# Fourteen matmul units of each half's mixing stage, regrouped into seven pairs with a seven product scheme

## The chip, the cores and the metric

One core of one Trainium2 chip runs the whole kernel in one launch. The metric is device time in microseconds (us), the median of the runs shown; a profile of one execution stands beside it. PE is TensorE (matrix multiply), PEld its weight loads, DVE is VectorE, ACT is ScalarE, POOL is GpSimd, SP is SyncE, whose queue issues most DMAs.

## The reference

One decoder layer on x (2048 tokens, 1024 features), all in float32:

```
u = rmsnorm(x, norm_mix_w);  proj = u @ w_in          # 1024 -> 2048 + 768 columns
q, f, v, g: 4 heads x 128 columns each;   att: 8 query heads, 2 key/value heads of 64
f = lb + (1 - lb) * sigmoid(f);  k = 1 - f;  q = q * 128**-0.5
S_t = diag(f_t) S_{t-1} + k_t v_t^T;  o_t = S_t^T q_t          # a recurrence per head
o_hg  = rmsnorm(o) * hg_norm_w * silu(g)
o_att = sliding window attention (128 keys back), with a sink logit per head
h = x + concat(o_hg, o_att) @ w_out
h = h + (silu(conv3(v2 @ w_gate)) * (v2 @ w_up)) @ w_down      # v2 = rmsnorm(h), d_ff = 2816
out = rmsnorm(h, final_norm_w)
```

## The kernel before

Everything lies transposed: features on 128 partitions, tokens along the free dimension. The 2048 tokens go in two halves (`hf`) of 1024. For each half there are four stages: the mix (projections, recurrence, attention), `out_proj`, `gate_up` and `down`. The first half's X is made in `head`, the second's at the end of the first half's `down`.

A float32 matrix product is made from three float32r products: an operand is split into a rounded `hi` (an ACT cast) and the rest `lo` (a DVE subtraction), and hi·hi, hi·lo and lo·hi are summed in PSUM. X, the eight K tiles of the normed input (128x1024 each), is held split in `xh`/`xl`.

`unit` (L204) is the plain projection of 128 columns: `prep` (L195) loads 512 KB of weights into `raw`, splits it into `whi`/`wlo`, and 8 K tiles x 3 products x 2 column halves = 48 matmuls of 128x512 fill two PSUM banks (line L222). In the mix of a half, 15 units run: `q` of attention (four, in `attend`, L493), `f` and `hq` of the recurrence (L586, L591; the `f` of head 0 is made earlier and comes in as `fu`), and `g`, the gate (L628). `project_v` (L782) makes the values of all four heads with 192 matmuls (L792 to L794) into one tile `v` of 16 KB a partition. PSUM has eight banks: four of kind `mm` for units, two `hg` for the recurrence, two `at` for attention.

`hgrn` (L584) is the recurrence of a head: seven doubling levels (L669 to L722), each with a multiply in place on DVE (L683), a gathering copy on ACT (L679) and small matmuls (L665), then the states (L743), the output (L757, L758), its norm and the gate. `QK`, `f`, `strip` and `SS` have one buffer each, so that the heads follow one another. `attend` (L491) is a pair of attention heads: scores (L520), masks (L529), exponentials (L542), transposes (L556) and outputs (L569). Both are generators that yield after each step. The string `ORDER` (L47) writes the order of the steps by hand: H0 is the next step of head 0, A1 of attention pair 1, W and V are the weights and the run of `project_v`, G1 the early weights of a gate, and S splits six of the eight tiles of the mix into operands for `out_proj`. The tile scheduler then places instructions by that priority: on PE, an instruction of an earlier step goes first as soon as it can, and a later one fills in where it can't. Tail: `out_proj` begins with the six tiles from S while head 3 and attention pair 3 finish.

Buffers: `raw` has three (`RAW`), `whi` and `wlo` two each. The pool `h` has eight 4 KB slots under the tag `m` (`slot`, L346), for the whole kernel; the six finished mix tiles wait in them until S.

`gate_up` already uses a seven product scheme (Strassen's, in Winograd's form) over all K tiles in `pair_unit` (L959), with its ACT copies of partial sums (L982).

## Time and profile before

| What | Value |
|---|---|
| three timed runs | 2113.6, 2114.18, 2114.54 us (median 2114.18) |
| span of the profiled execution, first to last instruction | 2112.5 us |
| PE, DVE, ACT busy over the span | 99%, 77%, 52% |
| mean TensorE clock granted | 0.999 |
| first half: mix from the end of the first `f` unit to the last mix instruction | 43.4 to 366.7 us |
| of it `project_v` | 65.9 to 111.5 us |

The page gives no time of its own for the profiled execution beside its span; the span lies 1.7 us under the median of the timed runs, for the start and the end of the launch. Times of instructions are from the span's start. A matmul's busy time overlaps with that of the next, so PE's pace is read from the time of many matmuls in a row and not from the mean of one.

### The profile page before, as it was taken

The page shows a single profiled execution, that of the slowest core. Times are in us where ns is not written, and L with a number is a line of the kernel's source. Part 1 is how long each engine was busy: PE and PEld are TensorE (multiplying, and loading weights), DVE is VectorE, ACT ScalarE, POOL GpSimd, SP SyncE. Part 2 cuts the span into 40 slices and gives each one's busy share as a digit, 9 for nine tenths or more (in the row PEclk, how much of TensorE's full clock was granted, in tenths as well). Part 3 has the DMA queues.
Part 4 walks back from the last instruction along what each step waited for, and adds up shares of the span by engine and source line. Part 5 has one row for each costly group of instructions (what it writes and reads, how often), then busy time and mean ns, then how long its engine had stood idle before and what let it go on. Part 6 is the DMA issues. An engine that isn't in the chain of part 4 may idle for free.

```text
span 2112.5 us, 29613 instructions
## 1 busy us (share of the span) xinstructions
PE 2098.0 (99%) x11480; PEld 1740.9 (82%) x11480; DVE 1624.3 (77%) x2355; ACT 1088.1 (52%) x1877; POOL 24.6 (1%) x52
## 2 busy tenths in 40 slices
PE   9999999999999999999999999999999999999998
PEld 7888888888888888888888888888888888888887
DVE  7457887898888878786773677868988788887766
ACT  6365565664444445345744566656544444444354
POOL 2000000000000000000000000000000000000000
PEclk9999999999999999999999999999999999999999
DMA  4111111513332325964641111214233233269643
GB/s 161 42 51 34 33 42 53 175 60 115 102 122 86 119 96 185 389 213 157 218 134 52 31 34 35 77 45 149 80 100 130 88 102 120 85 217 385 230 149 135
DMA packets 96617, 255.19 MB, mean 121 GB/s; under 512 B 17370, under 2 KB 19802, under 8 KB 96476
## 3 DMA queue, kind: packets, MB, share of 16 engines
q1 hardware_dynamic: 91220, 251.45, 34.9%
q10 hardware_dynamic: 5256, 1.85, 0.3%
q8 instruction: 90, 1.47, 0.3%
q14 instruction: 51, 0.42, 0.1%
HBM read 195.11 MB, written 57.16 MB: 119 GB/s over the span
## 4 chain that ended last, share of the span: by engine, by line
PE 96%; ACT 2%; DMA 1%; DVE 1%; issue 0%; SPq 0%; DVEq 0%
PE X L975 8%; PE X L976 8%; PE X L977 8%; PE pop L222 7%; PE hq L222 4%; PE q L222 4%; PE f L222 4%; PE pdx L1193 4%; PE pdx L1194 4%; PE pdx L1195 4%; PE Y L977 4%; PE Y L976 4%; PE Y L975 4%; PE g L222 3%; PE pdy L1194 3%; PE pdy L1193 3%
## 5 line engine op out<-in xcount | busy, mean ns | idle before, releaser
L800 ACT CAST whi<-raw 128x1024 fp32r<-128x1024 f32 x88 | 92.6, 1052 | 110.0 <-PE X L976 74.1
L975 PE MATMUL X<-T,whi 128*128 128x512 f32 x352 | 137.4, 390 | 0.0
L976 PE MATMUL X<-T,whi 128*128 128x512 f32 x352 | 137.0, 389 | 0.0
L977 PE MATMUL X<-T,wlo 128*128 128x512 f32 x352 | 137.0, 389 | 0.0
L1074 DVE SCALAR_TENSOR_TENSOR y<-ga,cw,y 128x1024 f32<-128x1024 f32 x88 | 112.3, 1278 | 25.7 <-ACT y L1072 25.7
L201 DVE TENSOR_TENSOR wlo<-raw,whi 128x1024 fp32r<-128x1024 f32 x57 | 69.3, 1218 | 60.8 <-ACT whi L200 60.5
L982 ACT COPY u<-X 128x512 f32<-128x512 f32 x88 | 51.6, 587 | 121.4 <-PE X L977 121.3
L801 DVE TENSOR_TENSOR wlo<-raw,whi 128x1024 fp32r<-128x1024 f32 x88 | 107.1, 1217 | 2.1 <-ACT whi L800 2.1
L200 ACT CAST whi<-raw 128x1024 fp32r<-128x1024 f32 x57 | 59.6, 1048 | 77.9 <-PE q L222 22.3
L222 PE MATMUL pop<-XL,whi 128*128 128x512 f32 x256 | 88.8, 391 | 0.0
L222 PE MATMUL pop<-XH,whi 128*128 128x512 f32 x256 | 88.0, 393 | 0.0
L222 PE MATMUL pop<-XH,wlo 128*128 128x512 f32 x256 | 87.1, 390 | 0.0
L801 DVE TENSOR_TENSOR xld<-raw,xhd 128x1024 fp32r<-128x1024 f32 x72 | 80.2, 1129 | 8.7 <-ACT xhd L800 8.6
L679 ACT COPY G<-QK 128x1024 f32<-128x1024 f32 x48 | 51.4, 1071 | 66.7 <-DVE QK L683 45.5
L800 ACT CAST xhd<-raw 128x1024 fp32r<-128x1024 f32 x72 | 68.9, 978 | 27.0 <-DMA raw<-act1B 6.0
L975 PEld LDWEIGHTS X<-T,whi 128*128 128x128 f32 x352 | 66.0, 188 | 15.1 <-ACT u L982 1.6
L977 PEld LDWEIGHTS X<-T,wlo 128*128 128x128 f32 x352 | 66.1, 188 | 13.8
L976 PEld LDWEIGHTS X<-T,whi 128*128 128x128 f32 x352 | 66.1, 188 | 13.7
L683 DVE TENSOR_TENSOR QK<-QK,f 128x1024 f32<-128x1024 f32 x56 | 68.5, 1223 | 11.3 <-ACT G L679 11.1
L1194 PE MATMUL pdx<-xld,hid 128*128 128x512 f32 x192 | 74.7, 389 | 0.0
L1193 PE MATMUL pdx<-xhd,hid 128*128 128x512 f32 x192 | 74.2, 390 | 0.0
L1195 PE MATMUL pdx<-xhd,lod 128*128 128x512 f32 x192 | 72.4, 389 | 0.0
(393 smaller groups left out, 6280.6 us busy)
## 6 DMA issues: line engine op xcount, KB each, us to landing
wr<-in_w_down SPq DMA_DIRECT2D x90, 512.0 KB
raw<-in_w_gate SPq DMA_DIRECT2D x44, 512.0 KB
raw<-in_w_up SPq DMA_DIRECT2D x44, 512.0 KB
raw<-act0T SPq DMA_DIRECT2D x20, 512.0 KB
raw<-act1T SPq DMA_DIRECT2D x20, 512.0 KB
act0B<-y SPq DMA_DIRECT2D x33, 256.0 KB
act1B<-y SPq DMA_DIRECT2D x33, 256.0 KB
raw<-in_w_out SPq DMA_DIRECT2D x16, 512.0 KB
```

The lines of the kernel that those rows point to most:

```text
L201: nc.vector.tensor_tensor(lo, raw, hi.bitcast(F32), op=ALU.subtract)
L222: marks["unit"] = nc.tensor.matmul(o[b], w, x[:, bs], start=f, stop=l)
L683: done = nc.vector.tensor_tensor(own, own, Fv.rearrange("p b w -> p w b").unsqueeze(3).to_broadcast([P, 2, nb, m]), op=ALU.mult)
L800: return (nc.scalar.copy(h, src), (eng or nc.vector).tensor_tensor(l, src, h.bitcast(F32), op=ALU.subtract))
L801: (eng or nc.vector).tensor_tensor(l, src, h.bitcast(F32), op=ALU.subtract))
L975: nc.tensor.matmul(o, wh[:, ws], xh, start=i == 0 and not more, stop=False, skip_group_check=more)
L976: nc.tensor.matmul(o, wh[:, ws], xl, start=False, stop=False, skip_group_check=more)
L977: r = nc.tensor.matmul(o, wl[:, ws], xh, start=False, stop=i == 3, skip_group_check=more)
L1074: nc.vector.scalar_tensor_tensor(y, g[:, w:w + HALF], C.cw[:, ft, w:w + 1], y, op0=ALU.mult, op1=ALU.add)
L1193: nc.tensor.matmul(o, wh[:, i, c], ah[:, i, cols], start=f, stop=False, skip_group_check=more)
L1194: nc.tensor.matmul(o, wh[:, i, c], al[:, i, cols], start=False, stop=False, skip_group_check=more)
L1195: nc.tensor.matmul(o, wl[:, i, c], ah[:, i, cols], start=False, stop=l, skip_group_check=more)
```

## The change

A pair of units with 256 output columns takes its first four K tiles as a 2x2 block product by seven products instead of eight, and its last four K tiles plainly. `Twofold` makes the combined halves of X once a half (T1 to T4, from X loaded anew), `two_units` runs a pair. The pairs are `q` of attention pair j with gate `g` of head j (four pairs), and `f` with `hq` of heads 1 to 3 (three pairs); `hq` of head 0 stays a plain unit. The gate is now made in `attend`, with ACT's Silu in place of a Sigmoid and a multiply. To make room, the slots `m` belong to each stage's pool (8 in the head, 5 in the mix, 8 in the rest), six finished mix tiles go to DRAM (`keep`) and come back at S, and the values of heads 1 to 3 go to DRAM and come back one at a time. The order is written anew, `project_v` now stands directly behind the unit of head 0. Core of the diff:

```diff
 ORDER = """
-H0 A0 H0 W0 V0 H0 G0 H0 A0 A0 H0 H0 H1 H0 H1 H1 H1 A0 A1 A0 G1 A1 A1 H1 H1 A1 A1 H2 H1 A2 H2 H2 H2 A2 H3 G2 A2 H2 A2 H2 A2 H2 A3 H3 H3 H3 A3 A3 H3 S A3 H3 A3 H3
+H0 W0 T0 H0 V0 U0 H0 A0 H0 H0 A0 A0 H0 H1 H0 H1 H1 H1 A1 H1 A0 A0 A1 A1 H1 H2 H1 A1 A1 H2 H2 H2 A2 H2 A2 A2 H2 H3 A2 A2 H2 H3 A3 H3 H3 A3 A3 H3 S A3 H3 A3 H3
 """
+DEEP = 2
+SLOTS = 5
+ROLES = ("XYZV", "ZYXV")
...
+    def keep(t, bs, name, kept, k):
+        if k not in kept:
+            kept[k] = dp.tile([P, HALF], F32, name=name)
+        nc.sync.dma_start(kept[k][:, bs], t[:, bs])
...
-        o = unit(a["w_att"][j], X, "q")
-        qT = slot(f"att{j}")
-        for b, bs in halves():
-            nc.vector.scalar_tensor_tensor(qT[:, bs], o[b], 0.125, invb[:, bs], op0=ALU.mult, op1=ALU.mult)
+        qT, g = slot(f"att{j}"), queries[j]
+
+        def scaled(bs):
+            nc.vector.scalar_tensor_tensor(qT[:, bs], qT[:, bs], 0.125, invb[:, bs], op0=ALU.mult, op1=ALU.mult)
             nc.scalar.activation(qT[:, bs], qT[:, bs], AF.Identity, bias=C.bq[:, j:j + 1])
+
+        def gated(bs):
+            nc.vector.tensor_tensor(g[:, bs], g[:, bs], invb[:, bs], op=ALU.mult)
+            nc.scalar.activation(g[:, bs], g[:, bs], AF.Silu)
+
+        two_units((a["w_att"][j], a["w_g"][j]), X, T, ((qT, scaled), (g, gated)))
...
-                mix[4 + j] = qT
+                keep(qT, gs, f"mix{hf}{4 + j}", mix, 4 + j)
...
+            two_units((a["w_f"][h], a["w_q"][h]), X, T, ((f, lambda bs: forget(bs, f[:, bs])),
+                                                         (q, lambda bs: scaled(bs, q[:, bs]))))
...
-        v = p.tile([P, HG, TT, P], F32, name="v")
+        v = [p.tile([P, TT, P], F32, tag=t, name=f"v{h}", bufs=n)
+             for h, (t, n) in enumerate((("v", 1), ("sc", 2), ("sc", 2), ("SS", 1)))]
...
-            nc.scalar.activation(v[:, :, tt], o.rearrange("p (h d) -> p h d", h=HG), AF.Identity,
-                                 scale=rs[:, tt:tt + 1])
+            for h in range(HG):
+                nc.scalar.activation(v[h][:, tt], o[:, h * P:(h + 1) * P], AF.Identity, scale=rs[:, tt:tt + 1])
+        away = {}
+        for h in range(1, HG):
+            away[h] = dp.tile([P, TT, P], F32, name=f"v{hf}{h}")
+            nc.sync.dma_start(away[h], v[h])
+
+        def values(h):
+            if h == 0:
+                return v[0]
+            t = p.tile([P, TT, P], F32, tag="v", name=f"v{h}", bufs=1)
+            nc.sync.dma_start(t, away[h])
+            return t
...
+    class Twofold:
...
+        def begin(self):
+            hf, p, lo, hi = self.hf, self.p, slice(0, 512), slice(512, HALF)
+            for i in range(DEEP):
+                x = []
+                for k in (i, i + DEEP):
+                    t = raw4(a["xT"][k, :, hf * HALF:(hf + 1) * HALF])
+                    nc.scalar.activation(t, t, AF.Identity, scale=nmw[:, k:k + 1])
+                    x.append(t)
+                x, y = x
+                t1 = p.tile([P, 512], F32, tag="pp", name="t1", bufs=4)
+                nc.vector.tensor_tensor(t1, x[:, hi], x[:, lo], op=ALU.subtract)
+                nc.vector.tensor_tensor(y[:, hi], y[:, hi], x[:, hi], op=ALU.subtract)
+                nc.vector.tensor_tensor(x[:, lo], y[:, hi], x[:, lo], op=ALU.add)
+                nc.vector.tensor_tensor(y[:, lo], y[:, lo], x[:, lo], op=ALU.subtract)
...
+                split_into(*both, y)
...
+                split_into(*self.t2[i], x[:, lo])
...
+        def end(self, X):
...
+                split_into(*self.ops["T1", i], self.t1[i])
+
+    def two_units(srcs, X, T, dst):
+        n = DEEP * P
+        r1, r2, S = raw4(srcs[0]), raw4(srcs[1]), raw4(None)
+        W = [[wp.tile([P, D], F32R, tag=t, name=f"w{t}", bufs=2) for t in ("hi", "lo")] for _ in range(3)]
+
+        def put(w, c, src):
+            split_into(*[t[:, c] for t in W[w]], src)
+
+        s1, s2, s3, s4 = [S[:, i * n:(i + 1) * n] for i in range(4)]
+        a11, a12, a21, a22 = [r[:, c] for r in (r1, r2) for c in (slice(0, n), slice(n, 2 * n))]
+        put(0, slice(0, 2 * n), r1[:, 0:2 * n])
+        nc.vector.tensor_tensor(s1, a21, a22, op=ALU.add)
+        nc.vector.tensor_tensor(s2, s1, a11, op=ALU.subtract)
+        put(0, slice(2 * n, 4 * n), S[:, 0:2 * n])
+        put(1, slice(0, D - 2 * n), r1[:, 2 * n:])
+        nc.vector.tensor_tensor(s3, a11, a21, op=ALU.subtract)
+        nc.vector.tensor_tensor(s4, a12, s2, op=ALU.subtract)
+        put(1, slice(D - 2 * n, D), S[:, 2 * n:])
+        put(2, slice(0, D - n), r2[:, n:])
+
+        b = {}
+        for r in ROLES[C.turn % 2]:
+            b[r] = ps("mm", r)
+        C.turn += 1
+        X1, Y, Z, V1 = b["X"], b["Y"], b["Z"], b["V"]
+
+        def terms(o, w, at, operands, start=False, stop=False):
+            wh, wl = W[w]
+            last = len(operands) - 1
+            for i, (xh, xl) in enumerate(operands):
+                c = slice(at + i * P, at + (i + 1) * P)
+                nc.tensor.matmul(o, wh[:, c], xh, start=start and i == 0, stop=False, skip_group_check=True)
+                nc.tensor.matmul(o, wh[:, c], xl, start=False, stop=False, skip_group_check=True)
+                nc.tensor.matmul(o, wl[:, c], xh, start=False, stop=stop and i == last, skip_group_check=True)
+
+        def deep(o, w, at, op, **k):
+            terms(o, w, at, [T.ops[op, i] for i in range(DEEP)], **k)
+
+        def plain(o, w, at, j, **k):
+            bs = slice(j * 512, (j + 1) * 512)
+            terms(o, w, at, [[t[:, bs] for t in X[kt]] for kt in range(2 * DEEP, KT)], **k)
...
+        def copied(i, j, o):
+            nc.scalar.copy(part(i, j), o)
+
+        def ready(i, j, o):
+            t = part(i, j)
+            nc.vector.tensor_tensor(t, t, o, op=ALU.add)
...
+        deep(X1, 0, 0, "B11", start=True, stop=True)
+        copied(0, 0, X1)
+        deep(Z, 0, n, "B21", start=True)
+        plain(Z, 1, 0, 0, stop=True)
+        ready(0, 0, Z)
+        done(0, 0)
+        deep(X1, 0, 3 * n, "T2", stop=True)
+        copied(0, 1, X1)
+        deep(Y, 0, 2 * n, "T1", start=True, stop=True)
+        copied(1, 1, Y)
+        deep(X1, 1, rest, "T3", stop=True)
+        copied(1, 0, X1)
+        deep(Y, 1, rest + n, "B22")
+        plain(Y, 1, 0, 1, stop=True)
+        ready(0, 1, Y)
+        done(0, 1)
+        plain(X1, 2, n, 1, stop=True)
+        ready(1, 1, X1)
+        done(1, 1)
+        deep(V1, 2, 0, "T4", start=True)
+        plain(V1, 2, n, 0, stop=True)
+        ready(1, 0, V1)
+        done(1, 0)
...
                     for kt in SPLIT:
-                        M[kt] = split(mix[kt])
+                        t = slot("mix")
+                        nc.sync.dma_start(t, mix[kt])
+                        M[kt] = split(t)
```

More of the change, by code (lines that the diff above doesn't have):

```diff
@@ L64, in hymba_layer @@
     wp = pool("w")
-    hp = pool("h")
     sp = pool("small", bufs=2)
@@ L439, in head @@
                 step(u, kt)
-        F = tuple(hp.tile([P, D], F32R, tag="m", name=f"w{t}", bufs=KT) for t in ("hi", "lo"))
+        F = tuple(m_tile([P, D], F32R, f"w{t}") for t in ("hi", "lo"))
         turn(cut, *F, raw[2], slice(0, D))
@@ L625, in hgrn @@
         nc.vector.tensor_tensor(strip, pd, C.ident.unsqueeze(1).to_broadcast([P, TT, 32]), op=ALU.mult)
-        def gate():
-            gu = unit(WG.get(h, a["w_g"][h]), X, "g")
-            for b, bs in halves():
-                nc.vector.tensor_tensor(q[:, bs], gu[b], invb[:, bs], op=ALU.mult)
-                nc.scalar.activation(gu[b], q[:, bs], AF.Sigmoid)
-                nc.vector.tensor_tensor(q[:, bs], q[:, bs], gu[b], op=ALU.mult)
-        if h == HG - 1:
-            gate()
-            yield
+        yield
         F, left, waiting = f, [], []
@@ L1289, in hymba_layer @@
     X = []
-    *nxt, summed = X, *head(X)
+    with ExitStack() as st:
+        home(pool("head", stack=st), KT)
+        *nxt, summed = X, *head(X)
     for hf in range(NH):
@@ L1294, in hymba_layer @@
             p = pool(f"mix{hf}", stack=st, reuse_waits="tile")
+            home(p, SLOTS)
+            T = Twofold(hf, p)
+            T.room()
+            p.tile([P, HALF], F32, tag="m", name="m", bufs=SLOTS)
             KS, V = att_keys(hf, kv, invb, p)
-            mix = [None] * KT
-            vs = []
-            M, WG = {}, {}
-            heads = [hgrn(hf, h, X, invb, vs, WG, mix, p, f0 if h == 0 else None) for h in range(HG)]
-            pairs = [attend(hf, j, X, invb, KS, V, mix, p) for j in range(ATT_J)]
-            wv = {}
+            mix, vs, M, queries, wv = {}, [], {}, {}, {}
+            heads = [hgrn(hf, h, X, T, invb, vs, mix, queries, p, f0 if h == 0 else None) for h in range(HG)]
+            pairs = [attend(hf, j, X, T, invb, KS, V, mix, queries, p) for j in range(ATT_J)]
             for n, step in enumerate(ORDER.split()):
```

73 lines of the change are left out of this document (51 added, 22 removed).

## The prediction

> **What bounds the kernel now.** I read the page first, then the chain that ended last, then busy times by stretch of the first half's mix, then the groups of DVE and ACT behind `project_v`, then single rows around the places that the change touches.
>
> ```profile
> span 2112.5 us, 29613 instructions
> PE 2098.0 (99%) x11480; PEld 1740.9 (82%) x11480; DVE 1624.3 (77%) x2355; ACT 1088.1 (52%) x1877; POOL 24.6 (1%) x52
> PE 96%; ACT 2%; DMA 1%; DVE 1%; issue 0%; SPq 0%; DVEq 0%
> ```
>
> PE is the bound by all three lines: busy nearly throughout, and 96% of the chain. But a busy PE need not run at its pace, so the chain's pieces give that: one unit is 48 matmuls.
>
> ```profile
> 32.52 10.92 PE f L222 x48
> 55.29 10.88 PE q L222 x48
> ...
> L975 PE MATMUL X<-T,whi 128*128 128x512 f32 x352 | 137.4, 390 | 0.0
> ```
>
> 10.88 us / 48 = 0.2267 us a matmul. That is the price of a matmul taken away in a dense stretch, not the 390 ns that single ones show in the page's groups, which overlap. The Trainium skill, "TensorE: Matmul & The Clock Gate", section "Back-to-back issue gap", gives about 131 ns a matmul for 512 columns in a real stream with weight loads. By it the change below would save 84 x 0.131 = 11.0 us and not 19.0; these rows disagree with it, and I go by them.
>
> Now the mix by stretches (us; then PE, PEld, DVE, ACT and POOL busy; clock; DMA share; GB/s). The first five are `hq` of head 0 with `q` of attention pair 0, `project_v`, the other units (the middle stretch), the last gate, and the tail; then the middle stretch of the second half, and two pieces of `gate_up`.
>
> ```profile
> 43.40:65.90 22.50, 22.50 (x105) 18.50 (x103) 15.17 (x18) 7.38 (x10) 1.61 (x3) 1.00 0.08 24
> 65.90:111.50 45.60, 45.60 (x274) 36.91 (x272) 15.53 (x24) 18.91 (x26) 0.00 (x0) 1.00 0.14 41
> 111.50:302.50 191.00, 191.00 (x1581) 161.13 (x1581) 138.85 (x287) 115.24 (x301) 6.05 (x9) 1.00 0.12 38
> 302.50:315.90 13.40, 13.40 (x78) 10.64 (x78) 13.01 (x16) 13.20 (x17) 0.00 (x0) 1.00 0.25 79
> 315.90:366.70 50.80, 49.55 (x477) 42.34 (x477) 37.21 (x84) 29.50 (x90) 0.00 (x0) 1.00 0.18 55
> 1158.00:1350.00 192.00, 192.00 (x1596) 162.23 (x1596) 139.59 (x282) 116.43 (x301) 6.04 (x9) 1.00 0.12 38
> 424.00:600.00 176.00, 176.00 (x776) 145.11 (x775) 153.28 (x203) 86.84 (x132) 0.00 (x0) 1.00 0.29 98
> 600.00:800.00 200.00, 200.00 (x884) 165.61 (x883) 166.41 (x211) 89.83 (x129) 0.00 (x0) 1.00 0.30 102
> ```
>
> PE waits for nothing before the tail, and there for 1.25 us. DVE is at 34% during `project_v`, 73% in the middle stretch, 73% in the tail; ACT at 60% in the middle. So matmuls removed from the mix are time removed, as long as DVE and ACT can feed what is left. In `gate_up` PE is full (200 us / 884 = 0.226 us a matmul) with DVE at 83 to 87%, on a scheme of the same kind.
>
> **Part 1: matmuls removed.** A pair as two units is 2 x 48 = 96. In `two_units` seven deep products have 2 K tiles x 3 = 6 each, 42, and four plain parts have 4 x 3 = 12 each, 48: 90. Six fewer a pair, 7 pairs a half, 2 halves: 84 x 0.2267 = **-19.0 us**. No other PE work changes.
>
> **Part 2: work added on DVE and ACT.** Prices:
>
> ```profile
> 30.99 2.36 DVE L201 TENSOR_TENSOR wlo<-raw,whi 128x1024 fp32r<-128x1024 f32 x2
> 1075.16 4.90 DVE L1286 TENSOR_TENSOR h<-h,sums 128x512 f32<-128x512 f32 x8
> L625 DVE TENSOR_TENSOR strip<-pdiag,ident 128x256 f32<-128x256 f32 x3 | 1.3, 421 | 7.2 <-PE pdiag L622 7.2
> L703 DVE TENSOR_TENSOR f<-f 128x256 f32<-128x256 f32 x3 | 1.9, 634 | 0.0
> L200 ACT CAST whi<-raw 128x1024 fp32r<-128x1024 f32 x21 | 21.9, 1049 | 25.4 <-PE q L222 11.1 <-issue 7.4 <-PE hq L222 4.0
> L731 ACT COPY Kn<-pkn 128x512 f32<-128x512 f32 x8 | 4.6, 587 | 0.0
> L631 ACT ACT_TABLE_LOAD x2 | 2.6, 1283 | 0.0
> ```
>
> In a row DVE takes 1.18 us for 1024 columns and 4.90/8 = 0.61 for 512; 768 I put between, 0.90. For 256 the rows give 0.42 and, strided, 0.63; mine are plain, and back to back a row costs less than alone, so 0.36 as an estimate. A pair now needs on DVE four `lo` splits of 512 and one of 768 (3.3), four sums s1 to s4 (1.4), four additions in `ready` and four multiplies (4.9): 9.7 us. Before, an attention pair's two units had two splits (2.4) and six multiplies (3.7), 6.0, since the gate had a second multiply; an `f`/`hq` pair had 2.4 + 2.4 = 4.8. So +3.6 for each of four and +4.9 for each of three: +29.1 us a half. `Twofold` adds 2 x (4 x 0.61 + 1.18 + 0.61) = 8.5 us in `begin` and 1.2 in `end`. `begin` is ordered ahead of `project_v`, during which DVE has 45.6 - 15.5 = 30 us free: hidden there, nothing on the path; without that cover 8.5 us a half.
>
> ACT: five casts (4 x 0.59 + 0.82) instead of two of 1.05, +1.1, and four copies of 0.59, +2.3: 3.4 us a pair, 24 us a half. Silu may want its own table: up to four loads of 1.28, 5 us. ACT behind `project_v` goes from (115.2 + 13.2 + 29.5)/255.2 = 62% to about 73%: no bound, but a longer queue.
>
> What DVE has behind `project_v`: before 138.9 + 13.0 + 37.2 = 189.1 us in 111.5 to 366.7 (255.2 us). After: 189.1 + 29.1 + 1.2 + 3.7 (the evacuation and first splits of `q` of pair 0, now behind `project_v`) - 4.8 (preparing the first pair during it) = 218.3. PE needs there 255.2 + 10.9 (that `q` unit, moved behind) - 7 x 1.36 = 256.6 us. So DVE would be at **85%**, the level of `gate_up`. A half breaks even when this stretch takes 256.6 + 9.5 = 266.1 us: DVE at 82%.
>
> **Part 3: hand-overs inside a pair.** One bank carries B11, T2, T3 and a plain part, and ACT must copy the bank out before the next group adds to it. Between T2's end and T3, and between T1's end and B22, stand 6 matmuls, 1.36 us. The copy takes 0.59; with one ACT instruction of 1.05 (row of L200) ahead of it, 1.64: 0.28 short. Twice a pair, 14 pairs: **+7.8 us**. Bounds: 0, as `gate_up` shows with such copies (over 12 matmuls there), or where other steps fill the gap; with two instructions ahead 1.33 short each, 37 us. I take the middle one: ACT at 73% mostly has something running, rarely a queue of two. The other hand-over, of weights: three `hi`/`lo` sets share two buffers. The third set has 24 matmuls (5.4 us) for a cast of 0.82, a split of 0.90 and one instruction ahead on each engine (2.2): hidden. The next pair's second set has 12 matmuls (2.7 us) for 0.59 + 0.61 + 2.2 = 3.4, 0.7 short, if pairs stood back to back: 10 us at most. But the middle stretch has 191 - 12 x 10.9 = 60 us of other matmuls, some 8 us a pair, to fill that: 0, and 10 as the bound.
>
> **Part 4: the start of `project_v`.** It now follows `hq` of head 0 directly, and its second weight part takes the buffer that this unit frees. Where that buffer came free before, ACT and DVE were in time as follows:
>
> ```profile
> 54.87 1.06 ACT L200 CAST whi<-raw 128x1024 fp32r<-128x1024 f32 x1 [3.97 <-PE hq L222]
> 55.10 1.29 DVE L594 SCALAR_TENSOR_TENSOR hg<-hq,invb 128x512 f32<-128x512 f32 x2 [3.94 <-PE hq L222]
> 56.31 1.21 DVE L201 TENSOR_TENSOR wlo<-raw,whi 128x1024 fp32r<-128x1024 f32 x1
> ```
>
> So `lo` is there at 57.5. PE is past `hq` at 55.3 and reaches that operand 8 matmuls later, 57.1: 0.4 to 0.6 us late a half, **+1.2 us** together. Bounds 0 (small matmuls fill it) and 2.3 a half (cast and split bare). The `q` unit of 10.88 us had covered it.
>
> **Part 5: DRAM.** A half stores three values and six mix tiles, loads them again, and loads four x tiles: some 11 MB over 310 us, 35 GB/s on top of 38, with the DMA engines at 12 to 14%. What a trip takes:
>
> ```profile
> 2.18 6.32 DMA x<-in_xT
> 322.07 5.68 DMA odd<-moved
> 272.71 40.27 SPq L192 DMA_DIRECT2D raw<-in_w_out  x4
> ```
>
> Store and load together are at most 2 x 6.3 = 12.6 us. The last mix tiles (head 2, attention 2) finish ahead of attention 3's pair, 90 x 0.2267 = 20.4 us of PE: hidden at S. Values of the next head load while that head does its levels: hidden. Stores wait in SP's queue for their tile, and weight loads stand behind them; the last row shows four loads spread over 40 us of waits for buffers without PE idling, so there is slack: 0. If a cover failed, 6 to 13 us once a half.
>
> **The sum.** -19.0 + 7.8 + 1.2 = -10.0. The span becomes 2102.5; the median of the runs lies 1.7 us above the span, so 2114.2 - 10.0 = **2104.2 us**.
>
> **Rivals.** *Hand-overs eat the gain.* If each of the 28 copies makes PE wait 0.64 us, 1.41 us of ACT work ahead of it instead of 1.05, the sum is -19.0 + 17.8 + 1.2 = 0: 2114.2. For it: 1.36 us of cover is half of `gate_up`'s, and ACT is fuller here (60% against 45 to 49%). Against: a later step's matmuls can fill, as they do in every gap of the mix today. The Trainium skill's "Perfetto Trace Analysis", section "Matmuls", speaks for this rival: independent groups should rotate through PSUM banks so that evacuation overlaps, and this scheme returns to one bank. In `gate_up` the trace shows that returning costs nothing with 12 matmuls between.
>
> *DVE and the recurrence become the bound: slower.* Behind `project_v`, DVE must work at 85% through chains that wait on ACT, PE and small DMAs. `gate_up` streams; the tail, all chains, got 73% and left PE idle. Its mechanism: heads follow one another through single buffers, each DVE step queues behind a pair's splits and sums, the chain of heads stretches, and PE runs out of units, since all four `mm` banks now belong to one pair. It decides from 82% down. At 80% the stretch takes 272.9 us, 6.8 over break-even, twice: 2127.8 us. Against it: PE had work without a pause while DVE had 27% free, so the free share shows no limit of the chains; in 302.5 to 315.9 DVE reached 97%.
>
> **How the numbers follow.** 0.2% is 4.2 us, about what a measurement of this kernel can tell from no change: faster is under 2110.0, slower over 2118.4. My forecast (2095 to 2110) has 0.66, the first rival 0.17, the second 0.17. The range starts at 2094, all hand-overs hidden (2114.2 - 19.0 = 2095.2) less 1 for the runs' spread (2113.6 to 2114.5), and ends at 2122, which takes in the first rival and the second down to DVE at 81%; about 0.15 is left out, most of it above. The likeliest case alone spans 2094 to 2110.
>
> **What would show it.** Right: 84 fewer PE instructions; the mix of each half some 5 us shorter; DVE at 83 to 85% behind `project_v`; PE idle in short waits on the ACT copies and nowhere for long. If PE stays full, I overrated Part 3. If the tail grows or PE waits behind `project_v` on DVE rows of the levels, the second rival holds. The forecast is wrong if `project_v` starts over 3 us late, or S waits for mix tiles from DRAM.

## The result, and the profile after

| | before | after |
|---|---|---|
| median of four timed runs | 2114.1 us (2113.6 to 2114.54) | 2177.56 us (2177.31 to 2178.81) |
| ratio | | 1.0302, 95% interval 1.0287 to 1.0316 |
| span of the profiled execution | 2112.5 us | 2175.6 us |
| mean TensorE clock granted | 0.999 | 0.986 |

The change made the kernel 63 us slower. The forecast was 10 us faster, and the range ended at 2122. Of run e16 below, one execution of four took 4363.14 us and is not counted.

The page of the changed kernel, the lines that answer to those of before:

```profile
span 2175.6 us, 29978 instructions
PE 2113.5 (97%) x11396; PEld 1744.6 (80%) x11396; DVE 1700.3 (78%) x2521; ACT 1169.4 (54%) x2055; POOL 24.3 (1%) x52
PE 78%; ACT 3%; DVE 2%; DMA 1%; issue 1%; ACTq 0%; DVEq 0%; SPq 0%
```

There are 11396 PE instructions, the 84 fewer that were counted. Yet the PE's idle time (span less busy) went from 14.5 to 62.1 us, and its busy time rose by 15.5 us although 19.0 us of matmuls were gone: 34.5 us more for the same work. As an estimate from the two mean clocks, 0.986 for 0.999 explains some 27 of them; the rest is not traced.

Busy time by stretches of the first half after the change (us; then PE, PEld, DVE, ACT, POOL; clock; DMA share; GB/s): `project_v`, the pairs up to 190, the pairs up to the last matmul of a pair, the tail, the last three together, and the same 176 us of `gate_up` that were shown of before:

```profile
54.70:99.40 44.70, 44.70 (x213) 36.19 (x213) 28.54 (x40) 24.11 (x48) 0.00 (x0) 1.00 0.22 71
99.40:190.00 90.60, 89.79 (x649) 73.64 (x648) 68.23 (x142) 60.05 (x139) 2.02 (x3) 1.00 0.24 81
190.00:332.80 142.80, 126.68 (x1080) 105.39 (x1077) 117.34 (x241) 101.50 (x245) 4.11 (x6) 0.92 0.22 74
332.80:382.10 49.30, 41.24 (x429) 34.33 (x427) 35.92 (x83) 32.07 (x94) 0.00 (x0) 0.97 0.09 28
99.40:382.10 282.70, 257.72 (x2151) 213.36 (x2150) 221.49 (x464) 193.62 (x476) 6.13 (x9) 0.95 0.20 68
...
451.60:627.60 176.00, 176.00 (x776) 145.10 (x775) 153.22 (x203) 86.88 (x132) 0.00 (x0) 1.00 0.29 98
```

`gate_up` is as it was, to a few hundredths of a us. All of the loss arises in the mix, and the first part of it lies there: from the end of `project_v` to the end of the tail it takes 282.7 us, where the prediction put the break-even at 266.1. DVE has 221.5 us of work there (218.3 were forecast), so its level is 78%. From 190 us on the PE is idle for 16.1 of 142.8 us, where before it had no pause up to 315.9.

A second part of the loss stands behind the tail. While head 3 and attention pair 3 finish, the PE fills in matmuls of the output projection; what it can't fill in follows as a dense run. The windows of these matmuls alone (tile `pop`), first half and second half, before:

```profile
366.70:424.00 57.30, 57.30 (x253) 47.11 (x251) 9.81 (x15) 1.00 0.46 161
1413.90:1471.30 57.40, 57.38 (x253) 47.15 (x252) 9.81 (x15) 1.00 0.45 161
```

and after:

```profile
382.10:451.60 69.50, 69.50 (x305) 56.98 (x305) 10.95 (x17) 1.00 0.50 171
1462.50:1534.40 71.90, 71.90 (x305) 58.92 (x305) 10.86 (x17) 0.96 0.41 136
```

52 matmuls fewer are filled in, 52 x 57.3 / 253 = 11.8 us a half. With the 16.6 us over break-even that makes 28.4 for the first half; its dense run ends at 451.6 against 424.0, 27.6 later. The second half loses 35.5 more (1534.4 against 1471.3, less 27.6).

What the PE waits for, over the whole run (total us, times, longest):

```profile
PE plev L685 <- ACT G L699: 13.3, 6, 7.1
PE psc L539 <- DVE sc L548: 7.8, 6, 3.0
PE X L903 <- ACT att L918: 4.0, 2, 2.9
...
PE X L903 <- ACT f L918: 2.1, 3, 0.8
...
PE Y L903 <- ACT hg L918: 0.9, 1, 0.9
```

The copies of partial sums (L918) are not at the head of the list: 7.0 us in the rows shown (a fourth row has 0.2 more). Ahead of them are waits in the recurrence and in attention, and before had 2.6 us of waits on `psc` as its largest row, and none on `plev`. The largest of all, in the PE's timeline (start, duration; idle time before it and its releaser in brackets):

```profile
273.51 0.41 PE L539 MATMUL psc<-KS,ql 128*128 128x256 f32 x1
280.99 2.12 PE L685 MATMUL plev<-G 128*64 128x64 f32 x48 [7.06 <-ACT G L699]
```

and what ACT did meanwhile:

```profile
273.82 1.05 ACT L699 COPY G<-QK 128x1024 f32<-128x1024 f32 x1
...
274.89 1.28 ACT L563 ACT_TABLE_LOAD   x1
276.18 0.21 ACT L563 ACTIVATE es<-es 128x8 f32<-128x8 f32 x1
...
278.99 0.38 ACT L561 ACTIVATE sc<-sc,m 128x128 f32<-128x128 f32 x1
...
279.89 1.05 ACT L699 COPY G<-QK 128x1024 f32<-128x1024 f32 x1
```

The level of the recurrence needs the copy `G`; in ACT's queue it stands behind a table load and eight exponentials of an attention pair (L561, the last at 278.99). The PE has nothing to fill in, although the pair of head 3 is only half done: the next of its matmuls (`X<-T20`, the product with T2) starts at 285.52. These rows show why:

```profile
250.30 0.39 PE L905 MATMUL X<-XH,wlo 128*128 128x512 f32 x1
...
281.57 1.22 DVE L703 TENSOR_TENSOR QK<-QK,f 128x1024 f32<-128x1024 f32 x1
282.82 0.59 ACT L918 COPY f<-X 128x512 f32<-128x512 f32 x1 [0.34 <-DVE QK L703]
...
285.52 0.78 PE L903 MATMUL X<-T20h,whi 128*128 128x512 f32 x1
```

The first product of the pair, B11, stands in its bank from 250.5 on. Its copy goes into `f`, and `f` has one buffer, which head 2 reads until its last level (L703, from 281.57). So the copy starts at 282.82, and the bank is held for 32 us. The rest of the pair hangs on it: T2, T3 and a plain part need this bank, and the third set of weights needs the buffer that T2 reads (its cast starts at 291.87). From 263.5 to 285.5 the PE is idle for 9.6 of 22 us. The pair of head 2 is held in the same way from 182.1 to 200.4, but there other matmuls fill in.

### The profile page after: what moved, and what is told of

It is laid out like the page before. It is cut to its first block, busy times and chain, and to the rows that moved or that the text cites. A ratio compares the mean times of both kernels' runs of the same rounds, so it can differ in the third digit from the quotient of the medians.

```text
span 2175.6 us, 29978 instructions
## 1 busy us (share of the span) xinstructions
PE 2113.5 (97%) x11396; PEld 1744.6 (80%) x11396; DVE 1700.3 (78%) x2521; ACT 1169.4 (54%) x2055; POOL 24.3 (1%) x52
## 4 chain that ended last, share of the span: by engine, by line
PE 78%; ACT 3%; DVE 2%; DMA 1%; issue 1%; ACTq 0%; DVEq 0%; SPq 0%
PE X L1128 7%; PE X L1129 7%; PE X L1130 7%; PE pop L230 7%; PE pdx L1346 4%; PE pdx L1347 4%; PE pdx L1348 4%; PE Y L1130 4%; PE Y L1129 4%; PE Y L1128 4%; PE pdy L1347 3%; PE pdy L1346 3%; PE pdy L1348 3%; PE Z L1130 2%; PE Z L1128 2%; PE Z L1129 2%
## 5 line engine op out<-in xcount | busy, mean ns | idle before, releaser
L953 ACT CAST whi<-raw 128x1024 fp32r<-128x1024 f32 (+2 forms) x158 | 136.7, 879 | 142.9 <-PE X L1129 74.4
L954 DVE TENSOR_TENSOR wlo<-raw,whi 128x1024 fp32r<-128x1024 f32 (+2 forms) x158 | 158.1, 1005 | 9.5 <-ACT whi L953 9.4
L703 DVE TENSOR_TENSOR QK<-QK,f 128x1024 f32<-128x1024 f32 x56 | 68.5, 1223 | 15.9 <-ACT G L699 15.8
L1130 PEld LDWEIGHTS X<-T,wlo 128*128 128x128 f32 x352 | 66.1, 188 | 13.8
L1130 PE MATMUL Y<-B,S 128*128 128x512 f32 x176 | 68.6, 390 | 0.0
L1130 PE MATMUL Z<-B,wlo 128*128 128x512 f32 x176 | 68.5, 389 | 0.0
L1128 PE MATMUL Y<-B,S 128*128 128x512 f32 x176 | 68.5, 389 | 0.0
```

The lines of the kernel that those rows point to most:

```text
L703: done = nc.vector.tensor_tensor(own, own, Fv.rearrange("p b w -> p w b").unsqueeze(3).to_broadcast([P, 2, nb, m]), op=ALU.mult)
L953: return (nc.scalar.copy(h, src), (eng or nc.vector).tensor_tensor(l, src, h.bitcast(F32), op=ALU.subtract))
L954: (eng or nc.vector).tensor_tensor(l, src, h.bitcast(F32), op=ALU.subtract))
L1128: nc.tensor.matmul(o, wh[:, ws], xh, start=i == 0 and not more, stop=False, skip_group_check=more)
L1130: r = nc.tensor.matmul(o, wl[:, ws], xh, start=False, stop=i == 3, skip_group_check=more)
```

## The experiments

Theories. LOAD: the added DVE and ACT work stretches the heads' chains. FILL: the pair's matmuls wait for copies and split weights while it holds all four `mm` banks. ORDER: the new order, the smaller room and the trips through DRAM cost the time, not the pairs. TABLES: Silu brings table loads. Two more came up on the way: POOLS (the slots belong to each stage) and CHAIN (a matmul saved ahead of the tail becomes idle time). Times are medians; the kernel before ran beside each at 2114.1 to 2114.6, and each ratio's interval is some 0.15% to either side, 3 us.

### Is it the pairs at all? (e1_units)

```diff
     def two_units(srcs, X, T, dst):
...
+        for src, (t, done) in zip(srcs, dst):
+            o = unit(src, X, "u")
+            for b, bs in halves():
+                done(bs, o[b])
```

> The changed kernel's ORDER, five slots, DRAM trips, heads' values in DRAM and Silu gate are kept; each pair is computed as two plain units of 48 matmuls one after the other, evacuated straight from PSUM, and the combined operands are not made (84 matmuls more than after, 11480 in all). Theory FILL (the pair's own matmuls wait for copies and split weights while it holds all four mm banks, so the in-order PE has nothing to put beside a head's chain) and theory LOAD (the added DVE and ACT work stretches the heads' chains): about 2114 to 2125 us, near before. Theory ORDER (the new order of steps, the five slots and the trips through DRAM cost the time): 2177.6 plus the 19 us of matmuls put back, some 2190 to 2197, or at the least above 2160. Theory TABLES (Silu costs 12 more table loads of 1.28 us, on the heads' chains): 2125 to 2140, since the Silu stays.

Measured: **2144.42** (ratio 1.0145, 1.013 to 1.016). All four theories gave another number. Without any pair the kernel already loses 30 us: order, room, trips and Silu together are nearly half of the loss, and the pairs the rest.

### Which part of order and room (e5_units_sigmoid, e8_order, e10_values, e11_eight_slots, e14_one_pool)

e5: plain units, the gate as before.

```diff
-            nc.scalar.activation(g[:, bs], g[:, bs], AF.Silu)
+            nc.scalar.activation(src, g[:, bs], AF.Sigmoid)
+            nc.vector.tensor_tensor(g[:, bs], g[:, bs], src, op=ALU.mult)
```

> The run of plain units (2144.4) with the gate as Sigmoid and a multiply, as before has it: what is left of the change is the order of the steps with q and g together, the five slots, the trips through DRAM. If the table loads of Silu cost here what they cost in the changed kernel (9.9), 2133 to 2137. If they only cost where DVE and ACT carry the pairs' work as well, 2142 to 2145. If this comes to 2114 to 2118, order and memory are innocent and Silu was all of the 30 us.

Measured: **2151.27**, 6.9 slower than with Silu and outside of all three expectations. Here Silu is a gain. A possible reason is that the Sigmoid keeps the PSUM bank until the multiply; that was not tried by itself, and the kernel before keeps it as long, where Silu is a loss (e6 below).

e8: before with the new ORDER, the gate behind `q` in `attend`; one pool of eight slots, nothing in DRAM.

```diff
-H0 A0 H0 W0 V0 H0 G0 H0 A0 A0 H0 H0 H1 H0 ...
+H0 W0 T0 H0 V0 U0 H0 A0 H0 H0 A0 A0 H0 H1 ...
...
+        two_units((a["w_att"][j], a["w_g"][j]), X, T, ((qT, scaled), (g, gated)))
```

> The kernel before with the changed kernel's order of steps alone: gate computed as a plain unit right behind q of attention, Sigmoid as before; eight slots, values and mix tiles in SBUF, no trip through DRAM, no pair. ORDER in the narrow sense (the gates, taken out of the heads, no longer stand beside the recurrence): as the run of plain units with Sigmoid, within 4 us of it, so 2130 to 2140. If it is the memory (five slots, values and mix tiles from DRAM): 2113 to 2119.

Measured: **2131.11** (1.0078, 1.0062 to 1.0094): the order alone costs 16.6 us. The windows of e8 up to its last unit and of its tail:

```profile
111.50:309.20 197.70, 197.70 (x1563) 166.32 (x1562) 142.92 (x282) 122.76 (x298) 5.60 (x9) 1.00 0.12 37
309.20:378.00 68.80, 60.21 (x571) 49.61 (x570) 50.99 (x110) 40.64 (x117) 0.00 (x0) 0.95 0.16 49
```

Up to the last unit the PE is as full as before, and the units end 6.7 us earlier than before's 315.9. But the tail is 68.8 us where before has 50.8, with 8.6 us of PE idle in place of 1.3. I read this as work that can cover the tail being spent early.

e10: e8 with the values of heads 1 to 3 in DRAM, as the change has them (`away[h]` and `values(h)` in `project_v`).

> The order run (2131.1: before with the new order alone, Sigmoid) plus one thing: the values of heads 1 to 3 go to DRAM and come back, with four head-wise evacuations in project_v and the tiles of sc and SS lent to them meanwhile. Eight slots, mix tiles in SBUF. Between it and the run of plain units with Sigmoid (2151.3) lie 20.2 us that the memory costs. Theory VALUES: most of it comes here, 2143 to 2151. Theory TAIL FILL (the mix tiles, kept in DRAM and read back through few slots, give the PE fewer output projection matmuls beside the last heads: 305 left for the dense run behind the tail against 253, 11.8 us a half): 2129 to 2135.

Measured: **2130.52**. The values' trip costs nothing that can be measured.

e11: e5 with `SLOTS = 8`, and without the room for the combined operands (`T.room()`).

> The run of plain units with Sigmoid (2151.3) with eight slots in place of five; trips through DRAM of values and mix tiles as there. TAIL FILL by the slots (the reads back wait until a slot is free): 2131 to 2140, and the dense run falls back to some 253 matmuls. TAIL FILL by the trip itself (the reads are issued too late whatever the slots): 2147 to 2152 with some 305 matmuls. VALUES: 2147 to 2152 as well, and the run with the values alone tells it apart.

Measured: **2149.74**, as e5 within the interval: not the number of slots. Its two dense runs are about as long as after's:

```profile
369.80:442.00 72.20, 71.08 (x309) 57.73 (x309) 10.96 (x17) 1.00 0.48 164
1433.30:1504.90 71.60, 70.84 (x308) 57.53 (x308) 10.95 (x17) 1.00 0.49 166
```

e14: e11 with the slots in one pool for all stages.

```diff
-            home(p, SLOTS)
...
-            home(p, KT)
+    home(pool("h"), KT)
```

> The run with eight slots (2149.7) with the slots in one pool for all stages, as before has them, in place of a pool for each stage; values and mix tiles still go to DRAM and come back, order and Sigmoid as there. The trace of that run has the loads of the third and fourth block of w_out and of the residual tiles at 374.6 us, behind the end of the mix, where the run with the values alone has them from 302 and 327 us on. Theory POOLS (the slots of the next stage lie in memory that the mix's tiles hold to the end, so that only two blocks of w_out can be prepared, and with them 79 matmuls in place of 131): 2129 to 2134, with some 253 matmuls left for the dense run. Theory TRIP (the way of the mix tiles through DRAM): 2146 to 2152.

Measured: **2136.48** (1.0108, 1.0091 to 1.0125): 13.3 us come back and 6.0 stay, so the result lies between the two expectations: POOLS is the larger part and TRIP (the mix tiles through DRAM) the smaller. The dense run of the second half is back at 253 matmuls (`1433.60:1491.20`, below), that of the first at 264. The casts of `w_out` on ACT show why, e11 first:

```profile
308.67 1.05 ACT L208 CAST whi<-raw 128x1024 fp32r<-128x1024 f32 x1 [1.79 <-PE u L230]
372.28 1.04 ACT L208 CAST whi<-raw 128x1024 fp32r<-128x1024 f32 x1
```

then e14:

```profile
308.62 1.05 ACT L208 CAST whi<-raw 128x1024 fp32r<-128x1024 f32 x1 [1.79 <-PE u L230]
332.82 1.05 ACT L208 CAST whi<-raw 128x1024 fp32r<-128x1024 f32 x1
```

```profile
1433.60:1491.20 57.60, 57.59 (x253) 47.38 (x253) 9.98 (x15) 1.00 0.46 160
```

The third block of weights is to be split into slots. With a pool for each stage these lie in memory that the mix holds to its end, and the cast stands until 372.28; with one pool it is done at 332.82, and the tail has something to fill in. The expectation named loads at 374.6 as the third and fourth block's; it is their casts that wait, and the loads at 374.6 are the next block's and the residual's.

### Table loads (e2_sigmoid, e6_before_silu)

e2: the changed kernel with the gate as Sigmoid into a tile and a multiply. e6: before with Silu in place of its Sigmoid and multiply.

> The changed kernel with the gate written as a Sigmoid into another tile and a multiply on DVE, as before has it, instead of one Silu; all else as after. TABLES: the 12 extra table loads (15.4 us) go, and the time falls by 10 us or more, to 2160 to 2168. FILL, LOAD, ORDER: within 5 us of after, 2172 to 2182 (LOAD gives the upper part, since DVE gets a multiply more for each bank of the gate).

> The kernel before with Silu for the gate in place of Sigmoid and a multiply on DVE, nothing else. TABLES as a cost of its own: 2120 to 2126 (12 more table loads, some 10 us of them on the heads' chains). If before's order hides them: 2113 to 2116, and then the 30 us of the load run are the elementwise work's.

Measured: e2 **2167.67**, 9.9 faster than after; e6 **2124.19** (1.0047, 1.0031 to 1.0063), 9.6 slower than before. Silu costs nearly the same in both. The table loads inside the mix, in the groups of ACT, of after and of before (count, busy us, mean ns):

```profile
L610 ACT ACT_TABLE_LOAD x12 | 15.4, 1283 | 0.2
L563 ACT ACT_TABLE_LOAD x12 | 15.4, 1283 | 0.2
L514 ACT ACT_TABLE_LOAD x8 | 10.3, 1283 | 0.1
```

```profile
L544 ACT ACT_TABLE_LOAD x10 | 12.8, 1283 | 0.2
L590 ACT ACT_TABLE_LOAD x6 | 7.7, 1283 | 0.1
...
L631 ACT ACT_TABLE_LOAD x4 | 5.1, 1283 | 0.1
```

32 against 20, as the expectation had it. Silu (L514) has its load, and the Sigmoid of the forget gate (L610), which stood beside the gate's Sigmoid in one set, needs its own as well. The Trainium skill, "ScalarE: Activation LUTs", section "Table sets: the hidden batching unit", says to batch by set and not by function; by the counts, Silu and Sigmoid are in different sets here.

That the number of loads sets the price is not shown. e6 was expected to have 12 loads more and has 4 (24), 5.1 us for a loss of 9.6. e1 has 26 and e5 20, and e1 is the faster by 6.9. e13 (below) has 34 and is no slower than e1 beyond the interval. Where a load falls counts, as in the 7.06 us above.

### What of the pairs costs (e4_load, e12_units_weights, e13_four_banks, e3_no_copies, e9_copies_beside)

e4: before with the pairs' elementwise work only.

```diff
+    def over(t, o):
+        nc.scalar.copy(t, o)
+        nc.vector.tensor_tensor(t, t, o, op=ALU.max)
...
+            over(qT[:, bs], o[b])
+            nc.vector.scalar_tensor_tensor(qT[:, bs], qT[:, bs], 0.125, ...
```

> The kernel before with the elementwise work of the pairs alone, on the same units: for f and q of heads 1 to 3, q of attention and all gates an ACT copy from PSUM and a DVE maximum that changes nothing ahead of the scaling, two DVE operations of 256 columns on each weight block, the split in two pieces and 768 columns of every second block split a second time, and Silu for the gate. Matmuls, banks and order are before's, so the time of the PE is before's. LOAD: DVE and ACT carry what they carry after, so the time rises to 2114.1 plus most of the 82 us that after lost beside its saving: 2160 to 2195. FILL and ORDER: 2114 to 2130. TABLES: 2125 to 2140.

Measured: **2144.33** (1.0143, 1.0128 to 1.0158), between the theories. If Silu costs here what it costs in e6, 9.6, the work itself costs some 20 us on the same matmuls and order. From `project_v` to the end of the tail:

```profile
111.50:388.00 276.50, 263.71 (x2154) 220.73 (x2153) 212.56 (x442) 184.66 (x455) 4.68 (x9) 0.99 0.14 41
```

Before has 189.1 us of DVE in 255.2 us, 74%. Here 212.6 of 276.5 are 77%: most of the added work became added time, though DVE had a quarter free.

e12: e1 with the weights' sums and splits and the combined operands. T1 is written over a half of two X tiles, as the pairs do it, so these units read it there in place of X. e13: e1 with four banks from the start and the results in the pairs' order (`some(0, 0, range(KT)); some(1, 1, range(4)); some(0, 1, range(KT)); ...`).

> The run of plain units (2144.4, Silu) plus the pairs' preparation: for each pair four DVE additions of 256 columns into a third block, the weights split in five pieces with 768 columns more, and the combined operands made and split as the pairs do, though no matmul reads them. Between plain units less 19 us of matmuls (2125.4) and the pairs without partial sums (2140.6) lie 15.2 us. LOAD: they are this work's, 2155 to 2162. FILL by four banks and late results: 2143 to 2148.

> The run of plain units (2144.4, Silu) with the two units of a pair taken together as the pairs do: four banks from the start, and the 96 matmuls in an order that completes the four results after matmul 24, 60, 72 and 96, as the pairs complete theirs after 24, 60, 72 and 90; in plain units both banks of the first result are complete after 48. No combined operand, no partial sum, no work added. FILL by four banks and late results: 2152 to 2162. LOAD: 2142 to 2147.

Measured: e12 **2153.76**, 9.3 slower than e1; e13 **2145.76**, 1.3 slower, inside the interval. FILL by banks and late results falls, for units that need no copies. The preparation counts in e12 somewhat less than LOAD gave.

e3: the pairs without copies and additions. e9: e3 with both put back as work on another tile, so that no matmul and no result waits for it.

```diff
-        copied(0, 0, X1)
...
-        ready(0, 0, Z)
-        done(0, 0)
+        done(0, 0, Z)
```

> The changed kernel's pairs without the partial sums: the 28 copies and 28 additions of a half between PSUM and the tiles are left out, and each result is scaled straight from its bank, so that what the copied products would have added to the result is left out of the output. All matmuls of the pairs, their weights' sums and splits, their banks and the order stay. FILL with the copies as the wait: the product that follows on the same bank no longer waits for ACT, so 2120 to 2145. FILL with the four banks and the split weights as the wait, not the copies: 2155 to 2172. LOAD: some 0.6 of the added DVE and ACT time goes, so 2130 to 2150. ORDER: 2170 to 2177.

> The run without partial sums (2140.6) with the 28 copies and 28 additions of a half put back as work beside it: an ACT copy of 512 columns and a DVE maximum of 512 columns at the same places in the order, on a tile of weight sums that is no longer needed, so that no matmul and no result waits for them. As there, the copied products are left out of the output. LOAD: most of the 37 us come back, 2165 to 2178. FILL (the waits of the bank and of the result for the copy): 2141 to 2150. In between, both count, in the proportion in which it stands.

Measured: e3 **2140.63** (1.013, 1.0113 to 1.0147), e9 **2159.14** (1.0217, 1.0199 to 1.0235), after 2177.56. The copies and additions cost 36.9 us: 18.5 as work put beside the pairs, and 18.4 more where the pairs depend on them, as waits, as banks held for `f`, and as the longer way of each result through its tile. Both theories count. The halves are rough, since something does wait in e9: the weight sums' tile is one of the three `raw`, it is given up later, and loads of weights stand in SP's queue for the maximum (L923; total us, times, longest). Loads wait for buffers in every one of these kernels, in e3 407.6 us for the splits alone, so this row need not have cost time; no run tells.

```profile
SPq L200 <- DVE raw L923: 38.1, 9, 8.6
```

### Were the 19 us to be had? (e16_units_fewer, e17_before_fewer)

```diff
                         for b, bs in both:
+                            if fewer and b and w is wl and kt in (1, 2, 3):
+                                continue
                             marks["unit"] = nc.tensor.matmul(o[b], w, x[:, bs], start=f, stop=l)
```

> The run of plain units (2144.4, Silu) with 84 matmuls fewer, at the pairs' places and without anything added: in each of the fourteen units of a half three of the 48 matmuls are left out (low part of the weights with K tiles 1 to 3, second bank), so their small terms miss from the output. Theory PE (a matmul less is 0.2267 us less, wherever it lies): 2125.4. Theory CHAIN (in this order and memory the chain of heads and attention sets the end of the mix, and a matmul saved ahead of it becomes idle time of PE in the tail): 2136 to 2144, the units end some 9.5 us earlier in each half and the dense run of output projection starts less than 4 us earlier.

> The kernel before with the same 84 matmuls left out at the same units, nothing else. PE: 2095.1, 19.0 us less. CHAIN: in before the tail is 51 us between the end of the units and the dense run, filled with 131 matmuls of the output projection; if the chain sets the end there too, 2104 to 2114, with PE idle time in the tail that before does not have.

Measured: e16 **2144.04** against e1's 2144.42, nothing saved; e17 **2105.03** (0.9956, 0.9941 to 0.9971), 9.2 saved of 19.0. The tails, from the end of the units to the dense run, first half, of e1:

```profile
313.70:368.10 54.40, 45.93 (x481) 37.89 (x479) 42.15 (x91) 37.83 (x100) 0.00 (x0) 0.94 0.18 61
```

and of e16:

```profile
299.60:366.80 67.20, 52.80 (x517) 43.76 (x515) 49.61 (x112) 43.01 (x120) 0.00 (x0) 0.85 0.18 58
```

The units end 14.1 us earlier and the dense run starts 1.3 earlier; the rest became a longer tail, with 14.4 us of PE idle in place of 8.5 and a lower clock. The dense run is the same 309 matmuls. In this order the chain of heads and attention sets the end of the mix, as CHAIN says. In before's order the units of e17 end at 307.3 in the first half, 8.6 earlier, and the dense run starts at 366.6, as before; there the gain comes from 19 matmuls more that are filled in. In the second half it is the other way round: the dense run has its 253 matmuls, and it starts 9.4 us earlier than before's, 4.1 of them from the first half. There 5.3 of the 9.5 us removed did shorten the mix:

```profile
366.60:419.90 53.30, 53.30 (x234) 43.85 (x234) 9.65 (x15) 1.00 0.52 173
1404.50:1462.10 57.60, 57.60 (x253) 47.40 (x253) 9.82 (x15) 1.00 0.46 160
```

### One repair (e15_shared_slots)

The changed kernel with Sigmoid, and five slots held in one pool through all stages (`if k < SLOTS: return hp.tile(...)` in `m_tile`).

> The changed kernel with Sigmoid (2167.7), and five slots that one pool holds through all stages, with three more in the stages outside the mix; pairs, order and trips as after. POOLS: the third and fourth block of w_out find slots before the mix ends, and the time falls by what the pools cost the plain units, some 19 us, to 2145 to 2153. If the slots come free too late for that (q and the attention's tiles still in them): 2160 to 2168. Below before's 2114 in no case.

Measured: **2173.39**, 5.7 slower than e2. POOLS does not carry over to the changed kernel. The dense runs shrink only to 293 and 277 matmuls, and the first tail is 57.7 us where e2's is 51.4. Why it is longer stays open. No run points to a version with pairs that beats before: even e3, which has no copies at all, is 1.3% over it.

### The account

| step | from, to (us) | cost |
|---|---|---|
| new order, gates behind `q` | before, e8 | +16.6 |
| values through DRAM | e8, e10 | -0.6 |
| mix tiles through DRAM | e10, e14 | +6.0 |
| slots by stage | e14, e11 | +13.3 |
| five slots for eight, room for the operands | e11, e5 | +1.5 |
| Silu for Sigmoid | e5, e1 | -6.9 |
| 84 matmuls fewer | e1, e16 | -0.4 |
| preparation, products, banks | e16, e3 | -3.4 |
| copies and additions as work | e3, e9 | +18.5 |
| the same as waits, held banks and longer way | e9, after | +18.4 |

They sum to 63.0, from 2114.55 to 2177.56. Steps below some 4.5 us (two intervals of 3 us taken together) can't be told from zero. The steps are not independent: Silu gains 6.9 here, and costs 9.9 once the pairs are there; preparation costs 9.3 on plain units and nothing clear of noise in its row. The account is one path, not a set of prices.

## Why the prediction was wrong, point by point

**Part 1, the step that failed first.** "So matmuls removed from the mix are time removed, as long as DVE and ACT can feed what is left." The count was right, 84, and the price was right where the PE is dense. But they were worth 9.2 us in before's order (e17) and nothing in the new one (e16). That the PE was full did not mean that it set the end of the mix: it was full because the output projection's matmuls and the units were spread over a chain of heads that is nearly as long. The sign was there in the rows quoted: the 50.8 us of tail, in which the PE's fill was work of the next stage. The chain that ended last shows it too, when it is read for that tail alone and not over the run, where PE has 96%: from 315.4 to 331.0 it runs through ACT, DVE and a small DMA, the 5.68 us of `odd<-moved` that Part 5 quotes, and only then on the PE.

**The order and the room were costed at nothing.** The prediction priced the start of `project_v` and the DRAM trips; it had no term for the moved gates or for slots that belong to a stage. Without any pair these came to 36.7 us with the Sigmoid (e5), and to 30 with Silu (e1). The change's string ORDER was read for what moves past `project_v`, not for what is left to cover the tail.

**Part 2.** The added DVE work was right (221.5 us against 218.3). "DVE would be at 85%, the level of `gate_up`" failed: it reached 78%, and 77% in e4. `gate_up` is no measure for a stretch of chains. ACT at 73% was near the 68% measured, but on ACT the queue's order counts more than the share: see the 7.06 us above. Silu was given four table loads a half and no time; it has six more a half, and 9.9 us in all (e2).

**Part 3.** 7.8 us were forecast for hand-overs inside a pair, at most 37. The waits put down to the copies are 7.0 us in the rows shown, and that this is the size forecast is luck, as it is that 36.9 us lies at the bound of 37. The step took ACT's queue for all that a copy waits for, 1.64 us at the most likely. It left out the copy's target: with one buffer of `f`, the bank of B11 was held 32 us for head 3 and 18 for head 2, and the PE's idle time then stands under other names (`plev`). Taking the copies out gives 36.9 us: as work they lengthen ACT's and DVE's queues ahead of the heads' steps, and they hold banks and delay each result. The work was left to Part 2's level, where it was lost.

**Part 4.** +1.2 was forecast; `project_v` runs from 54.70 without a pause, and the PE waits for nothing there: 0. (It takes 44.7 us against 45.6, with 213 matmuls in it against 274.)

**Part 5.** Values: 0, as forecast (e10). Mix tiles: 0 was forecast and 6.0 measured (e14 against e10). In the second half of after the cover failed; the chain that ended last runs through the store and the load:

```profile
1410.91 4.18 DMA mix<-hg
1415.15 3.68 DMA mix<-mix
```

7.9 us, in the bounds of 6 to 13 given for that case.

**The rivals.** The second, "DVE and the recurrence become the bound: slower", was right in sign and in place: PE waits on rows of the levels and of attention, with no matmuls of a unit to put in. Its break-even of 82% held, with 78% reached. Its price was too small: at 78% its own formula gives 218.3 / 0.78 - 266.1 = 13.8 us a half, 27.6 in all, and the 11.8 us a half of output projection that is no longer filled in was not in it. It gave as the reason that all four banks belong to one pair. By itself that costs nothing (e13); with the copies one of the four stood full, and so the reason is partly right. Its chance of 0.17 was too low: the tail at 73% with the PE idle was the nearest row to the new stretch, and I went by `gate_up`.

**What stays open.** Why Silu gains in e1; why preparation costs 9.3 us in e12 and nothing between e16 and e3; how the 18.4 us divide between the matmuls' waits, the bank held for `f` and the longer way of the results (a second buffer of `f` was not tried); whether the second half's further 8 us (35.5 against 27.6) are the mix tiles' trip of 7.9 or also the lower clock of its dense run, 0.96.

## What to carry to other kernels

A PE that is busy all the time may still be off the path: look at what it is busy with where the stage ends, and take the matmuls out alone, with nothing added, before building a scheme that saves them. Before a copy is to free a bank, see that its target is free too. When buffers are given to a stage, see which later stage's early loads and splits used them as cover. And price elementwise work on a chained stretch by that stretch's own level, not by a streaming stage's.

## What the runs showed of the hardware

Idle time of the PE costs more than its length, since the clock falls behind it. The changed kernel shows it twice around the 7.06 us gap. The first time the clock is at half before that gap:

```profile
270.00:274.00 4.00, 3.09 (x72) 2.73 (x72) 3.92 (x14) 1.39 (x5) 0.00 (x0) 0.50 0.08 16
```

Ahead of this window lie gaps of 0.76 and 1.67 us, with four small matmuls between them; the clock over 265 to 270 is 0.98. It stays at half through the gap of 7.06 us and until about 286.5. The second time, in matmuls of 512 columns that should start 0.2267 us apart:

```profile
286.89 0.40 PE L903 MATMUL X<-T21h,whi 128*128 128x512 f32 x1
287.13 0.39 PE L904 MATMUL X<-T21l,whi 128*128 128x512 f32 x1
...
292.73 0.50 PE L903 MATMUL V<-T430h,whi 128*128 128x512 f32 x1 [1.97 <-ACT whi L953]
293.07 0.40 PE L904 MATMUL V<-T430l,whi 128*128 128x512 f32 x1
293.30 0.41 PE L903 MATMUL X<-T430h,whi 128*128 128x512 f32 x1
...
294.31 0.63 PE L903 MATMUL X<-T431h,whi 128*128 128x512 f32 x1
294.74 0.63 PE L904 MATMUL X<-T431l,whi 128*128 128x512 f32 x1
```

At 286.89 they are 0.24 us apart, the full pace; a gap of 1.97 us follows; at 293.07 the pace is still 0.23, and from 294.31 on it is 0.43. The Trainium skill, "TensorE: Matmul & The Clock Gate", section "What's actually happening", has the clock halved after an idle window of about 3.4 us; here gaps of 1.67 and 1.97 us were enough, so the rows do not agree with a pause of that length as the condition. The Trainium skill, on the same page in section "Wait — 56ns, not 53.3ns?", gives 426.7 ns for 512 columns on a cold array; the 0.43 us agree.

ACT's table load takes 1.283 us, and the next ACTIVATE starts right behind it (274.89 + 1.28, 276.18). The Trainium skill's "ScalarE: Activation LUTs", section "What ACT_TABLE_LOAD costs", gives 1283 ns and some 1380 ns of drain with it; the drain does not show in these rows, where the copy before the load ends at 273.82 + 1.05 = 274.87.
